# The first store of a split-SiLU kernel as four transfers: partitions by fours, two rows first

## The chip, the cores and the metric

One core of a Trainium2 chip runs the whole program. The metric is the device time of one execution in microseconds (us); eleven executions of the kernel before, in the rounds of e1 to e4, lie between 470.30 and 471.67 us, within 0.3%. Each kernel was also run once under the hardware profiler, and the tables here come from that run. A run more than 1.5% above the fastest of its kernel is called slow and isn't compared.

## The reference

```python
# x: (32, 512, 2048) float32
x1, x2 = x[..., :1024], x[..., 1024:]
out = x1 * (1 / (1 + np.exp(-x1))) * x2      # float32, (32, 512, 1024)
```

That is 134.2 MB in, 67.1 MB out, and two cheap elementwise steps.

## The kernel before

The 16384 rows are cut into 16 tiles of 128 partitions with 8 rows each. A tile is one load of 8 MB (64 KB per partition, in one piece), one silu on ScalarE (ACT), one multiply on VectorE (DVE), and one store of 4 MB (32 KB per partition). SP issues the loads, ACT the stores. There are two input and two output buffers. The first tile is computed in four chunks of two rows, the last is computed and stored in four chunks.

```python
    in_pool = ctx.enter_context(tc.tile_pool(name="in_pool", bufs=2))
    out_pool = ctx.enter_context(tc.tile_pool(name="out_pool", bufs=2))
    ...
    load(0)
    load(1)
    for i in range(n_tiles):
        xt = loaded.pop(i)
        ov = view(out_flat, i)
        ot = out_pool.tile([P, K, half], dt, name="ot")
        if i < n_tiles - 1:
            kc = KC_EDGE if i == 0 else K          # KC_EDGE = 2, K = 8
            for c in range(0, K, kc):
                silu(ot, xt, c, c + kc)            # ACT
                mul(ot, xt, c, c + kc)             # DVE, in place
            nc.scalar.dma_start(out=ov, in_=ot)    # 4 MB
            if i + 2 < n_tiles:
                load(i + 2)                        # 8 MB, nc.sync
            continue
        ...                                        # last tile: four quarters
```

Of the kernel before, what the change touches and what calls it, by code (L numbers as in the profile page):

```python
# [1 line left out]

# [4 lines left out]


def issue_ahead_of_the_first_barrier(nc):




    head, body = nc.main_func.blocks[:2]
    load = next(ins for ins in body.instructions if type(ins).__name__ == "InstDMACopy")
    at = next(
        j for j, ins in enumerate(head.instructions)
        if ins.engine == load.engine and type(ins).__name__ == "InstDrain"
    )
    body.instructions = [ins for ins in body.instructions if ins.name != load.name]  # L20
    head.instructions = head.instructions[:at] + [load] + head.instructions[at:]


@with_exitstack
def kernel(
    ctx: ExitStack,
    tc: tile.TileContext,
    x: bass.AP,
    out: bass.AP,
):  # L30






    nc = tc.nc
    P = nc.NUM_PARTITIONS

    x_flat = x.flatten_outer_dims()  # L40
    out_flat = out.flatten_outer_dims()
    num_rows, in_cols = x_flat.shape
    half = in_cols // 2
    dt = x_flat.dtype

    K = 8
    KC_EDGE = 2
    PLAN = [K] * (num_rows // (P * K))

    in_pool = ctx.enter_context(tc.tile_pool(name="in_pool", bufs=2))  # L50
    out_pool = ctx.enter_context(tc.tile_pool(name="out_pool", bufs=2))

    plan = []
    row = 0
    for k in PLAN:
        plan.append((row, k))
        row += P * k
    assert row == num_rows
    n_tiles = len(plan)

    def view(flat, i):
        row0, k = plan[i]
        return flat[row0:row0 + P * k].rearrange("(p k) d -> p k d", k=k)

    nc.at_finalize(issue_ahead_of_the_first_barrier)


    ctx.enter_context(tc.manual_schedule())

    loaded = {}  # L70

    def load(i):
        xt = in_pool.tile([P, K, in_cols], dt, name="xt")
        nc.sync.dma_start(out=xt[:, :plan[i][1], :], in_=view(x_flat, i))
        loaded[i] = xt

    def silu(ot, xt, c, ce):
        nc.scalar.activation(  # L78
            out=ot[:, c:ce, :],
            in_=xt[:, c:ce, :half],  # L80
            func=mybir.ActivationFunctionType.Silu,
        )

    def mul(ot, xt, c, ce):
        nc.vector.tensor_mul(  # L85
            out=ot[:, c:ce, :],
            in0=ot[:, c:ce, :],
            in1=xt[:, c:ce, half:],
# [9 lines that stand above are left out]
            kc = KC_EDGE if i == 0 else K  # L98
            for c in range(0, K, kc):
                silu(ot, xt, c, c + kc)  # L100
                mul(ot, xt, c, c + kc)
            nc.scalar.dma_start(out=ov, in_=ot)
            if i + 2 < n_tiles:
                load(i + 2)
            continue

        cuts = list(range(0, K, KC_EDGE))
        for n, c in enumerate(cuts + [None, None]):
            if c is not None:
                silu(ot, xt, c, c + KC_EDGE)  # L110
                mul(ot, xt, c, c + KC_EDGE)
            if n >= 2:
                b = cuts[n - 2]
                nc.scalar.dma_start(out=ov[:, b:b + KC_EDGE, :], in_=ot[:, b:b + KC_EDGE, :])


# [1 line left out]
_INS = ['x']  # L118
_OUTS = [((32, 512, 1024), 'float32')]


# [23 lines left out]
```

## Time and profile before

| | before |
|---|---|
| device time, median of 4 runs | 470.56 us |
| span in the profile | 468.6 us |
| loads, stores: share of 16 DMA engines | 66.4%, 33.2% |
| silu of a whole tile, multiply of a whole tile | 7.03 us, 8.69 us |
| distance from tile to tile | 29.0 us |

A tile's silu and multiply take 15.7 us one after the other and fit beside its 29 us; the DMA engines are what is full, at 66.4 + 33.2 = 99.6% of their time. The lines are read in the prediction below. The timeline of the kernel before shows when its first store is issued and when silu of tiles 1 and 2 starts (start, length, engine, line):

```profile
32.70 0.38 ACTq L102 DMA_DIRECT2D out_dram<-ot  x1
44.84 7.03 ACT L78 ACTIVATE ot<-xt 128x8192 f32<-128x8192 f32 x1 [15.70 <-DMA xt<-in_x_dram]
73.81 7.03 ACT L78 ACTIVATE ot<-xt 128x8192 f32<-128x8192 f32 x1 [21.94 <-DMA xt<-in_x_dram]
```

One more view will be needed, the records of single DMA packets in the trace. In them a *packet* is one partition's piece of one transfer (2048 packets of 64 KB for 16 loads of 128 partitions). I sorted them into turns: groups of 16 packets of one queue and size, which I take as one for each of the 16 engines. L64 is a load packet of 64 KB, S32 a store packet of 32 KB, "done" a 4-byte write of 9 ns. Each transfer has 16 of these behind its data (256 for 16 loads, 304 for 19 stores), and I call them its completion: silu of tile 2 starts at 73.81 us, 0.5 us after the last one of load 2 at 73.30. This is the kernel before, with the first and last start of a turn and the shortest, median and longest packet in ns:

```
 61.82.. 62.42  S32   1213 1213 1213
 63.03.. 63.63  L64   2418 2418 2418
 65.44.. 66.04  S done   (store 0)
 65.45.. 66.05  L64   2418 2418 2418
 67.86.. 68.46  S32   1213 1213 1213
 69.07.. 69.67  L64   2418 2418 2418
 71.48.. 72.09  S32   1213 1213 1213
 72.69.. 73.30  L done   (load 2)
 72.70.. 73.30  S32   1213 1213 1213
```

The two queues alternate packet by packet here, a completion write is a turn as well (store 0's at 65.44 us stands alone between the load packets of 63.03 and 65.45), and all 16 engines do the same within 0.6 us.

### The profile page before, as it was taken

Reading aid. Unit: us, or ns where it says so; the run is one execution under the profiler, and the core shown is the slowest. Engines: PE = TensorE matmul, PEld = TensorE weight load, DVE = VectorE, ACT = ScalarE, POOL = GpSimd, SP = SyncE. Lnnn points to the kernel's source line nnn. Section 1 sums busy time; section 2 is a strip of 40 time slices with the busy share of each in tenths; the row PEclk is TensorE's granted clock in tenths of the full one; section 3 lists DMA queues with packets and bytes.
Section 4 is the critical chain, followed back from the end, with each engine's and each line's share of the span. In section 5 each row is a group of like instructions: output and inputs, shape, how many; then the busy total and the mean of one; then the engine's idle time right before and its main releaser. Section 6 shows DMA issues by size and latency. Waiting matters only on the chain.

```text
span 468.6 us, 183 instructions
## 1 busy us (share of the span) xinstructions
DVE 139.5 (30%) x22; ACT 114.3 (24%) x23; POOL 0.2 (0%) x4
## 2 busy tenths in 40 slices
DVE  0070510606115060250702407024070330703333
ACT  1141405023050230503205032050410504105050
POOL 0000000000000000000000000000000000000000
DMA  9899999999999998998999999999999999999998
GB/s 442 386 425 403 439 456 448 403 417 434 448 448 403 448 470 380 448 481 380 481 400 420 478 448 403 403 448 448 448 403 445 434 420 448 431 420 492 394 411 358
DMA packets 5040, 201.33 MB, mean 430 GB/s; under 512 B 560, under 2 KB 560, under 8 KB 560
## 3 DMA queue, kind: packets, MB, share of 16 engines
q1 hardware_dynamic: 2304, 134.22, 66.4%
q10 hardware_dynamic: 2736, 67.11, 33.2%
HBM read 134.22 MB, written 67.11 MB: 430 GB/s over the span
## 4 chain that ended last, share of the span: by engine, by line
DMA 72%; DVE 14%; ACT 11%; DVEq 0%; issue 0%; ACTq 0%
DMA xt<-in_x_dram 72%; DVE ot L85 14%; ACT ot L78 11%; DVEq L140 0%; ACTq L78 0%
## 5 line engine op out<-in xcount | busy, mean ns | idle before, releaser
L85 DVE TENSOR_TENSOR ot<-ot,xt 128x8192 f32<-128x8192 f32 (+1 forms) x22 | 139.5, 6362 | 322.1 <-ACT ot L78 322.1
L78 ACT ACTIVATE ot<-xt 128x8192 f32<-128x8192 f32 (+1 forms) x22 | 113.0, 5163 | 343.0 <-DMA xt<-in_x_dram 343.0
L78 ACT ACT_TABLE_LOAD x1 | 1.3, 1283 | 0.8 <-PEq L129 0.8
L129 POOL MEMSET const-bfloat16-1.0<- 128x1 bf16 x1 | 0.1, 101 | 0.0
L129 POOL MEMSET const-uint8-127<- 128x1 uint8 x1 | 0.1, 101 | 0.0
L129 POOL MEMSET const-float32-0.0<- 128x1 f32 x1 | 0.1, 98 | 0.2 <-issue 0.2
L129 POOL MEMSET const-float32-1.0<- 128x1 f32 x1 | 0.1, 98 | 0.0
## 6 DMA issues: line engine op xcount, KB each, us to landing
out_dram<-ot ACTq DMA_DIRECT2D x15, 4096.0 KB, 34.7
out_dram<-ot ACTq DMA_DIRECT2D x4, 1024.0 KB, 5.7
xt<-in_x_dram SPq DMA_DIRECT2D x16, 42.1
```

What stands on the lines that cost most here:

```text
L78: nc.scalar.activation(out=ot[:, c:ce, :], in_=xt[:, c:ce, :half], func=mybir.ActivationFunctionType.Silu,)
L85: nc.vector.tensor_mul(out=ot[:, c:ce, :], in0=ot[:, c:ce, :], in1=xt[:, c:ce, half:],)
L129: nc = _bacc.Bacc("TRN2", target_bir_lowering=False, num_devices=1)
```

## The change

The intent: the first store begins with small packets and takes more turns, so that the loads get ahead, and the step from loads alone to loads and stores is gentler.

```diff
+    OPENING = [
+        (slice(0, None, 4), slice(0, 2)),
+        (slice(0, None, 4), slice(2, None)),
+        (slice(2, None, 4), slice(None)),
+        (slice(1, None, 2), slice(None)),
+    ]
...
-            nc.scalar.dma_start(out=ov, in_=ot)
+
+            for ps, ks in OPENING if i == 0 else [(slice(None), slice(None))]:
+                nc.scalar.dma_start(out=ov[ps, ks], in_=ot[ps, ks])
```

## The prediction

What rests on nothing that a trace of this case shows is cut from the text on record, and each cut is marked: one paragraph, the first rival (that the choice of partitions makes store packets longer) with the places in the range, the chances and the signs that lean on it, and two guesses at the cause of the slow turn. The sum came to 470.57 - 0.5 + 0.1 = 470.2 us. The -0.5 is the author's estimate, about half of the 1.1 us that the trace shows, and the +0.1 one from the small packets of the tail. The range was 469.5 to 470.9 us without the first rival, and the 0.02 for slower by 2% was for that rival.

> **What bounds the kernel now.** I read the page first: who is busy, and what its chain says.
>
> ```profile
> span 468.6 us, 183 instructions
> ...
> DVE 139.5 (30%) x22; ACT 114.3 (24%) x23; POOL 0.2 (0%) x4
> ...
> q1 hardware_dynamic: 2304, 134.22, 66.4%
> q10 hardware_dynamic: 2736, 67.11, 33.2%
> ...
> DMA 72%; DVE 14%; ACT 11%; DVEq 0%; issue 0%; ACTq 0%
> ```
>
> The compute engines work under a third of the span. Queue q1 carries the loads (issued by SP), q10 the stores (issued by ACT); together their packets fill 66.4 + 33.2 = 99.6% of the time of all 16 DMA engines. The chain gives 25% to DVE and ACT, but a chain is only what released what. To see whether the engines ever ran dry, I cut the span where the traffic changes kind and asked for the DMA share of each stretch (last two columns: share, GB/s).
>
> ```profile
> 0.00:0.90 0.90, 0.00 (x0) 0.12 (x1) 0.20 (x4) 1.00 0.00 0
> 0.90:4.00 3.10, 0.00 (x0) 1.16 (x1) 0.00 (x0) 1.00 0.99 338
> 4.00:35.30 31.30, 8.90 (x4) 7.31 (x4) 0.00 (x0) 1.00 1.01 436
> 35.30:38.80 3.50, 0.00 (x0) 0.00 (x0) 0.00 (x0) 1.00 0.99 300
> 38.80:449.50 410.70, 121.69 (x14) 98.41 (x14) 0.00 (x0) 1.00 1.00 434
> 449.50:456.80 7.30, 4.13 (x2) 6.07 (x4) 0.00 (x0) 1.00 1.00 431
> 456.80:467.10 10.30, 4.77 (x3) 1.24 (x1) 0.00 (x0) 1.00 0.96 407
> 467.10:468.60 1.50, 0.00 (x0) 0.00 (x0) 0.00 (x0) 1.00 0.00 0
> ```
>
> From 0.9 us until the last data at about 467 us the share is 1.00 within the rounding of a packet that crosses a cut. Loads alone (4 to 35 us), loads and stores mixed (39 to 449) and stores alone (449 to 457) all move at 431 to 436 GB/s. (The 407 of the last row comes from a window that ends 0.2 us late and starts late by a packet; 4.19 MB at 434 GB/s are 9.7 us.) So the end is fixed by bytes over one rate: 201.33 MB / 434 GB/s = 463.9 us, plus about 1 us before the first packet, 1.5 us from the last data to the end, and two slow packets. Those two are the first load packets (338 GB/s) and the load packets in flight when the **first store** arrives (300 GB/s): 3.5 x (1 - 300/434) = 1.1 us. The second is the only DMA time that a different first store can recover. The sum, 463.9 + 1 + 1.5 + 0.7 + 1.1 = 468.2, is the span within 0.4.
>
> How the two queues share an engine is seen in one short window just after the first store has come in (queue, packets, MB, share):
>
> ```profile
> DMA packets 32, 1.57 MB, mean 437 GB/s; under 512 B 0, under 2 KB 0, under 8 KB 0
> ...
> q1 hardware_dynamic: 16, 1.05, 67.2%
> q10 hardware_dynamic: 16, 0.52, 33.7%
> ```
>
> That is 38.8 to 42.4 us: every one of the 16 engines took one load packet (64 KB, 2.42 us) and one store packet (32 KB, 1.21 us). A turn is a packet, whatever its size. This is the lever of the change.
>
> [...]
>
> **The change, part by part.** The same 4 MB leave from the same buffer after the same compute; nothing is loaded, computed or issued earlier: the first piece is issued where the whole store was, at 32.70 us. Added: three issues on ACT, about 3 x 0.36 us by the timeline's duration of such an issue, in a stretch where ACT waits for load 1 until 44.84, so hidden. Packets: per engine 8 become 10 (2 of 8 KB, 2 of 24 KB, 6 of 32 KB), and 4 completion writes in place of 1. Small packets cost little: the tail moves its 4 MB in 8 KB packets in about 9.8 us against 9.7 at full rate, 0.1 us for 24 more packets per engine, so 2 more are worth 0.01 us. I allow 0.1 us for all of this.
>
> What moves is the **order**. A completion write takes a turn too (two load packets in succession are seen at 63.0 and 65.4 us, where store 0's completion lies between them). The first store thus takes 14 turns in place of 9, and load packets fill the turns in between. Counted turn by turn from 38.86 us, the start of the first store packet (my estimate, from 2.418, 1.213, 0.91 and 0.31 us for 64, 32, 24 and 8 KB):
>
> - load 1 has one packet left; it ends 0.9 us sooner, since an 8 KB packet stands ahead of it in place of 32 KB. Silu of tile 1 starts near 43.9 in place of 44.84.
> - load 2's completion comes after 9 load packets, 21.8 us, and stores of 0.62 + 1.82 + 4 x 1.21 = 7.3 us: near 67.9, so it lands near 69.0 in place of 73.8.
> - store 0's completion comes after its own 9.7 us and 11 load packets, 26.6 us: near 75.2, where it was at 65.5. It lands near 76.1 in place of 66.4.
>
> The output pool has two buffers, and tile 2 takes the one of tile 0. Its silu will therefore wait for **store 0** (76.1), no longer for load 2 (69.0): 2.3 us later than the 73.81 of now. From there every tile keeps one turn for one turn, so loads stay some 4.8 us ahead, stores some 10 us behind, and each tile's silu waits for the store two back. That looks like a new bound and is none: the engines stay full as long as either queue has work. Load 4 goes out 15.8 us after silu 2 starts (7.0 silu + 8.7 multiply), near 92, while load 3 lasts to near 96; and store 1, issued near 60, lasts past 100. At the end, load 15 lands near 446 in place of 450.7; silu of tile 15 waits for store 13 until about 449.3; the first quarter of the last store is issued near 453.6 (455.0 now), while store 14's eight packets keep the engines to about 458. Today the same handover, store 14's last packet to the first quarter, meets within 0.1 us near 457. So the change adds slack there, with nothing to recover.
>
> The sum: bytes and rate 0; fragments +0.1; the slow turn at the first store between -1.1 and 0. A smaller first packet (8 KB, a quarter) may shorten that turn [...]; I take -0.5. 470.57 - 0.5 + 0.1 = 470.2 us.
>
> **Rivals.** [...] (2) *The new wait starves the DMA.* If loads were issued too late, q1 would run dry; but then q10, with a store and a half queued, runs at the same 434 GB/s. Both would have to be empty. Small. (3) *The tail gains.* A handover gap of a microsecond at 457 would be closed by the longer store queue; the trace shows 431 GB/s up to 456.8 and no hole, so there is no more than 0.1 us. (4) *The whole slow turn goes*: 469.5.
>
> **Range and chances.** Measured runs of before spread over 470.44 to 471.02. [...] 8 in 10: 469.2 to 471.8. Faster by 2% would need 9.4 us, and all DMA time outside bytes over rate is about 5 us, so 0.005. Slower by 2% [...]: 0.02. The rest, 0.975, is within 2%.
>
> **What would show it right or wrong.** The DMA share stays 1.00 in every stretch and 434 GB/s from 39 us on. Silu of tile 1 starts near 44, that of tile 2 near 76; in the view of waits, ACT's waits for loads of x are largely replaced by waits for stores of ot, and the chain names stores. Load 15 lands some 4 to 5 us earlier, the end doesn't move. The stretch around the first store shows whether 300 GB/s has risen. I'm wrong if store packets of 32 KB take clearly over 1.21 us near 45 to 75 us [...], if a stretch shows a DMA share under 0.95, or if the spacing of tiles leaves 29.0 us.

## The result, and the profile after

The changed kernel took 470.57 us (median of 4 runs, 470.31 to 470.69) against 470.56 us. The ratio is 0.9996, with an interval of 0.9981 to 1.0011. Ratios here are the mean time of one kernel's fast runs over that of the other's of the same rounds, so not quite the ratio of the medians. Both profiled runs were fast ones.

The page of the changed kernel shows 80 more packets on the store queue: 2 more data packets and 3 more completion writes for each of 16 engines.

```profile
span 468.5 us, 188 instructions
...
q1 hardware_dynamic: 2304, 134.22, 66.4%
q10 hardware_dynamic: 2816, 67.11, 33.2%
```

The same stretches as in the prediction, for the changed kernel:

```profile
35.30:38.80 3.50, 0.00 (x0) 0.00 (x0) 0.00 (x0) 1.00 0.86 300
38.80:449.50 410.70, 121.69 (x14) 99.65 (x15) 0.00 (x0) 1.00 1.00 433
449.50:456.80 7.30, 6.60 (x3) 6.07 (x4) 0.00 (x0) 1.00 1.00 432
```

The first row is a lesson in reading. The 300 GB/s is the same as before, because a packet counts where it starts, and in both kernels just 16 load packets start in these 3.5 us. The share tells them apart: 0.99 x 3.5 = 3.5 us is the length of one slow load packet before, 0.86 x 3.5 = 3.0 us that of one after. The packet records have 3436 and 2990 ns as the medians, where an ordinary load packet takes 2418. So the slow turn went from 1.02 us over to 0.57.

The timeline of the changed kernel around the first store (start, length, engine, line):

```profile
23.82 8.90 DVE L91 TENSOR_TENSOR ot<-ot,xt 128x2048 f32<-128x2048 f32 x4 [23.82 <-ACT ot L84]
26.15 0.55 ACTq L110 DMA_DIRECT2D out_dram<-ot  x1
27.30 1.89 ACT L84 ACTIVATE ot<-xt 128x2048 f32<-128x2048 f32 x1
32.75 0.33 SPq L80 DMA_DIRECT2D xt<-in_x_dram  x1
32.75 1.78 ACTq L110 DMA_DIRECT2D out_dram<-ot  x3
44.34 7.03 ACT L84 ACTIVATE ot<-xt 128x8192 f32<-128x8192 f32 x1 [15.15 <-DMA xt<-in_x_dram]
51.40 8.69 DVE L91 TENSOR_TENSOR ot<-ot,xt 128x8192 f32<-128x8192 f32 x1 [18.68 <-ACT ot L84]
60.13 0.36 ACTq L110 DMA_DIRECT2D out_dram<-ot  x1
71.27 7.03 ACT L84 ACTIVATE ot<-xt 128x8192 f32<-128x8192 f32 x1 [19.90 <-DMA xt<-in_x_dram]
```

The first piece goes out at 26.15 us and not at 32.7: it holds rows 0 and 1 alone, which the first of the four multiplies finishes (23.82 + 2.29 = 26.11 us), so it waits for that one only. The other three go out where the whole store went before. Its packets of 8 KB run from 30.7 us, when loads are still alone. Silu of tile 2 starts at 71.27, 2.5 us sooner than before (73.81); silu of tile 15 at 448.26 and not 450.73. The data end at 467.13 us in the packet records, before at 467.37. The 2.5 us lead of the loads is not in the end time, because the stores are behind by as much work: after the last load, store 14 has all 8 packets per engine to send, where it had 6 left before.

### The profile page after: what moved, and what is told of

Its sections match the earlier page's. It is cut to its first block, busy times and chain, and to the rows that moved or that the text cites. A ratio compares the mean times of both kernels' runs of the same rounds, so it can differ in the third digit from the quotient of the medians.

```text
span 468.5 us, 188 instructions
## 1 busy us (share of the span) xinstructions
DVE 139.5 (30%) x22; ACT 114.3 (24%) x23; POOL 0.2 (0%) x4
## 4 chain that ended last, share of the span: by engine, by line
DMA 72%; DVE 14%; ACT 11%; DVEq 0%; issue 0%; ACTq 0%
DMA xt<-in_x_dram 72%; DVE ot L91 14%; ACT ot L84 11%; DVEq L148 0%; ACTq L84 0%
## 5 line engine op out<-in xcount | busy, mean ns | idle before, releaser
L91 DVE TENSOR_TENSOR ot<-ot,xt 128x8192 f32<-128x8192 f32 (+1 forms) x22 | 139.5, 6362 | 319.6 <-ACT ot L84 319.6
L84 ACT ACTIVATE ot<-xt 128x8192 f32<-128x8192 f32 (+1 forms) x22 | 113.0, 5163 | 340.5 <-DMA xt<-in_x_dram 340.5
```

What stands on the lines that cost most here:

```text
L84: nc.scalar.activation(out=ot[:, c:ce, :], in_=xt[:, c:ce, :half], func=mybir.ActivationFunctionType.Silu,)
L91: nc.vector.tensor_mul(out=ot[:, c:ce, :], in0=ot[:, c:ce, :], in1=xt[:, c:ce, half:],)
```

## The experiments

Twelve kernels ran. I call **offset** the number of load packets between the completion of a load and the next completion of a store, counted in the turns of one tile after another. A tile has 8 load packets, so it runs from 0 to 8. It is 6 in the kernel before (above: "S done" comes two load packets ahead of "L done"), and 8 in the changed kernel, where the store's completion takes the turn just ahead of the load's. The first eight kernels were made without this idea, the last four because of it. The medians are over all runs, and those of e3, e5 and e8 include one slow run; the ratios are of fast runs alone. The intervals of e5, e7, x2 and x4 lie clear of 1.

| kernel | median, us | ratio to before (95%) | offset |
|---|---|---|---|
| e1_after: the changed kernel again | 470.66 | 0.9995 (0.9983 to 1.0007) | 8 |
| e2_late4: four pieces, none early | 470.61 | 0.9994 (0.9982 to 1.0007) | 2 |
| e3_rows: 2 rows, then 6, all partitions | 471.06 | 1.0009 (0.9987 to 1.0030) | 3, then mostly 0 |
| e4_contig: neighbouring partitions | 470.61 | 0.9993 (0.9980 to 1.0006) | 8 |
| e5_less_load: half of load 7 left out | 465.08 | 0.9853 (0.9827 to 0.9879) | 8, then 0 |
| e6_half_mul: half of the multiplies | 470.73 | 0.9994 (0.9981 to 1.0007) | 8 |
| e7_store0_late: first store 8 us later | 480.10 | 1.0198 (1.0185 to 1.0212) | 1 |
| e8_all_four: every store in four pieces | 497.50 | 1.0555 (1.0523 to 1.0587) | changing |
| x1_late_two: e7, first store in halves | 470.95 | 1.0005 (0.9990 to 1.0020) | 2 |
| x2_three_late: three pieces, none early | 480.63 | 1.0210 (1.0193 to 1.0227) | 1 |
| x3_halves: first store in halves | 470.79 | 1.0004 (0.9990 to 1.0019) | 7 |
| x4_back: x2, then store 5 in halves | 476.08 | 1.0112 (1.0091 to 1.0133) | 1, later mostly 2 |

### e1_after

No edit: the changed kernel again, in five rounds.

> The changed kernel once more, in five rounds, to narrow the interval. Theory (the 16 DMA engines are full from the first packet to the last, so only the slow turn at the first store can be won): the data end 0.2 to 0.3 us sooner in the two traces, so the ratio is 0.9990 to 1.0000, silu of tile 1 near 44.3 and of tile 2 near 71.3. Rival (the earlier start of the first store is a real gain of a microsecond that four runs could not resolve): ratio 0.998 or less.

0.9995 with an interval of 0.9983 to 1.0007: no gain that five rounds can resolve, and none of a microsecond and more would have hidden. Silu of tile 1 starts at 44.54, of tile 2 at 71.47.

### e2_late4

```diff
-        (slice(0, None, 4), slice(0, 2)),
-        (slice(0, None, 4), slice(2, None)),
+        (slice(0, None, 4), slice(6, 8)),
+        (slice(0, None, 4), slice(0, 6)),
```

> The same four pieces, but the first holds rows 6 and 7, which are ready last, so that none can be issued before 32.7 us. This is what the prediction assumed. Theory: the turn count of the prediction holds here: silu of tile 2 near 76 us, released by store 0 and no longer by load 2 (which lands near 69); time within 0.3% of the kernel before. The slow load packet near 36 us: at most as long as in the changed kernel (3.0 us) if a small first store packet shortens it, 3.4 us if not. Rival (early issue is what keeps the changed kernel level, and fragments cost): this one is slower by 1 us or more.

Level, 470.61 us. This is the kernel that the prediction had in mind, and its turn count comes out. The timeline of e2:

```profile
32.85 2.50 ACTq L110 DMA_DIRECT2D out_dram<-ot  x4
42.12 7.03 ACT L84 ACTIVATE ot<-xt 128x8192 f32<-128x8192 f32 x1 [12.83 <-DMA xt<-in_x_dram]
...
57.90 0.36 ACTq L110 DMA_DIRECT2D out_dram<-ot  x1
75.70 7.03 ACT L84 ACTIVATE ot<-xt 128x8192 f32<-128x8192 f32 x1 [26.55 <-DMA out_dram<-ot]
```

Silu of tile 2 waits for store 0 and starts at 75.70 (76.1 predicted). In the packet records load 2 completes from 67.6 us on (67.9 predicted), store 0 from 74.9 (75.2 predicted). Only silu of tile 1 is off: 42.12, where 43.9 was predicted, because the count forgot the second 8 KB packet, which saves another 0.9 us (309 ns in place of 1213), and the shorter slow turn saves the rest. ACT now spends its waiting on stores, as the waits of e2 show, and the end is where it was:

```profile
ACT ot L84 <- DMA out_dram<-ot: 307.4, 14, 26.6
ACT ot L84 <- DMA xt<-in_x_dram: 32.8, 2, 19.9
```

307 us of waiting for another transfer, and not 0.1% in the time: here a wait of an engine that isn't the bound changed its name for nothing. The long load packet at the first store is spread over two turns here (2516 ns at 35.5 us, 2807 at 41.2, in the median), 0.49 us over in all, with nothing issued early. So a small first packet was enough to make the slow turn shorter (0.49 us over, 1.02 in the kernel before); what the slow turn is, I didn't find.

### e3_rows

```diff
-    OPENING = [... four pieces ...]
+    OPENING = [
+        (slice(None), slice(0, 2)),
+        (slice(None), slice(2, None)),
+    ]
```

> Two transfers, no striding: rows 0 and 1 of all partitions, issued near 26 us, then rows 2 to 7. 16 packets per engine (8 of 8 KB, 8 of 24 KB). Theory: time within 0.3% of both kernels; first store packets near 30.7 us as in the changed kernel; early issue comes from the rows and not from the partitions. More turns in the early stretch (8 small packets each with a load packet between), so store 0 lands later than in the changed kernel, silu of tile 2 after 75 us. Rival (the strided partitions matter): this differs from the changed kernel by more than 1 us.

Fast runs: 473.42, 470.49, 470.46, 471.64, 470.43, and a slow one of 482.72. 473.42 stands out. The profile is of that run. In it only 28 load packets after 60 us take over 2.5 us, but one engine falls 2 us behind the others near 67 us and a few later on, and the end waits for the last: the last store's completion writes run from 466.6 to 470.1 us, against 466.8 to 467.4 in the kernel before. The first piece was issued at 26.42, as expected, and silu of tile 2 started at 80.00. So load 4 was issued only at 95.8 us, as load 3 was ending, and on most engines stores took the turns until it came: this is where offset 3 ended.

Which engines lose time after that can be followed, since on an engine each packet starts within a few ns of the end of the one before it (3 to 5 ns in the kernel before, from 60 to 440 us). Twelve engines went on at offset 0 and one at 2; none of their load packets took over 2.5 us between 104 us and the end. Three engines were at offset 1 for a part of the run, and 26 of the 28 slow packets are theirs, mostly one per tile. The two that were at offset 1 from about 244 us on lost 1.8 and 2.1 us between 232 and 440 us. So in this run engines at offset 1 fell behind even though the others were not at it.

### e4_contig

```diff
+        (slice(0, 32), slice(0, 2)),
+        (slice(0, 32), slice(2, None)),
+        (slice(32, 64), slice(None)),
+        (slice(64, 128), slice(None)),
```

> The same four pieces by size, over neighbouring partitions: 0 to 31 (2 rows, then 6), 32 to 63, 64 to 127. [...] Rival (an engine's rate is all that counts, whichever partitions it reads): packets stay at 1.21 us and the time within 0.3%.

Level, 470.61 us, and every 32 KB packet of partitions 32 to 63 and of 64 to 127 took 1213 ns, as in the kernel before. The theory had longer store packets for neighbouring partitions; no trace shows what it rested on. With these packets it falls, so does rival (1) of the prediction, and with them the reason I had seen for the stride of four. Which partitions a piece holds made no difference here; how many packets and pieces there are, does, as x2 will show (2.1%). That is for store packets between load packets; a store of 64 partitions alone wasn't run.

### e5_less_load

```diff
-        nc.sync.dma_start(out=xt[:, :plan[i][1], :], in_=view(x_flat, i))
+        kl = K // 2 if i == 7 else K
+        nc.sync.dma_start(out=xt[:, :kl, :], in_=view(x_flat, i)[:, :kl, :])
```

(Tile 7 is then computed in halves, both from the rows that were loaded. The result is wrong.)

> The changed kernel with only half of tile 7 loaded (4.19 MB less; the compute of tile 7 uses the half that is there twice, so the result is wrong on purpose). Theory (bytes over 434 GB/s set the end): 9.7 us less, so near 460.9 us, ratio near 0.979. Rival (the compute on the chain of waits sets a part of the end): the saving is under 7 us.

The fast runs were 461.96, 465.19 and 464.97; the kernel before had a median of 471.17 us in these rounds. By the ratio that is 6.9 us less, where 9.7 was expected; one run alone comes near, 9.2 us less. The interval, 5.7 to 8.2 us less, leaves the 9.7 out, so the theory's number failed. By the letter the rival ("under 7 us") has it, but e6 speaks against its reason, and what took the rest is open. The profile (469.77 us) isn't compared. What it shows by itself is a warning: the short load moved the offset from 8 to 0, and from there on the engines were up to 4 us apart and many load packets longer than 2418 ns (the page has 432 GB/s in the mean of slices 3 to 20 and 419 in that of 21 to 39, all of them nine tenths busy or more).

### e6_half_mul

```diff
-                mul(ot, xt, c, c + kc)
+                mul(ot, xt, c, c + (kc if i == 0 else K // 2))
```

(A wrong result.)

> The changed kernel with VectorE multiplying only half the rows of tiles 1 to 14 (wrong result on purpose). The chain of waits gives DVE 14% of the span, and this takes about 4.3 us out of each of 14 tiles, 60 us in all. Theory: the end stays within 0.3%, since loads and stores are only issued earlier into queues that are already full. Rival (the chain is the bound): every second tile lies on the chain, so some 30 us less.

```profile
span 468.6 us, 188 instructions
...
DVE 79.7 (17%) x22; ACT 114.3 (24%) x23; POOL 0.2 (0%) x4
```

DVE lost 59.8 us of work (139.5 to 79.7), and the span is 468.6. The chain's 14% for DVE was worth nothing: the chain is a path, and the DMA queues beside it were full (share 1.00, 433 GB/s from 76 to 449 us).

### e7_store0_late

The kernel before, with the first store moved behind silu of tile 1:

```diff
                 silu(ot, xt, c, c + kc)
+                if i == 1:
+                    nc.scalar.dma_start(out=first[0], in_=first[1])
                 mul(ot, xt, c, c + kc)
-            nc.scalar.dma_start(out=ov, in_=ot)
+            if i == 0:
+                first = (ov, ot)
+            else:
+                nc.scalar.dma_start(out=ov, in_=ot)
```

> The kernel before, with the whole first store held back until ACT has started silu of tile 1, so issued near 45 us and not at 32.7. Theory: loads run alone in the meantime at the same rate, so the time is within 0.3%; tile 2 waits for store 0. The slow load packet moves with the store, to about 47 to 50 us, and is again near 3.4 us, since the first store packet is 32 KB. Rival for the slow packet (it belongs to the issue of load 2 at 32.7 us): it stays near 35.5 us. Rival for the time (the earlier first store is worth what it is earlier): 10 us slower.

Here the theory failed: 480.10 us, 2% slower. The rival for the time named nearly this number ("10 us slower") for another reason, which x1 will test. On the slow packet the theory held: it moved with the store, to 42.8 us, and was again 3438 ns. (47 to 50 was expected: the store was issued at 41.11 and not near 45, since load 1, alone on the engines, ended sooner.)

From 76 to 449 us the DMA engines of e7 are as busy as those of the kernel before, and move less. First row the kernel before, second e7:

```profile
76.00:449.00 373.00, 113.00 (x13) 89.19 (x13) 0.00 (x0) 1.00 1.00 434
```

```profile
76.00:449.00 373.00, 112.99 (x13) 89.10 (x13) 0.00 (x0) 1.00 1.00 427
```

Share 1.00 in both. A packet's time is busy time also when the packet is slow, so a full share, here with 434 and 427 GB/s, is no proof of a full rate. In the packet records of e7 the load packets are slow and the engines drift apart (columns as above):

```
 98.25.. 98.92  L done   (load 3)
 99.47..100.14  L64   2418 2418 2418
101.88..102.55  S done   (store 1)
101.89..102.56  L64   2418 2542 2716
104.30..105.21  S32   1213 1213 1213
105.51..106.42  L64   2418 2528 2625
```

375 load packets of 2048 took over 2.5 us (32 in the kernel before, all of them in the first and the slow turn); the excess over 2418 ns sums to 7.9 us per engine, against 1.7. Tiles are 29.57 us apart (silu at 102.88 and, eleven tiles on, at 428.10), against 28.99.

### e8_all_four

```diff
-            for ps, ks in OPENING if i == 0 else [(slice(None), slice(None))]:
+            for ps, ks in OPENING:
```

> The changed kernel with all 15 stores of 4 MB in the same four pieces: measures what fragments cost, and drives the stores behind the loads tile after tile. Theory: 30 more packets per engine and 45 more completion writes cost at most 0.1 us a tile, so 0 to 1.5 us slower; loads fall dry at times, and the DMA share stays 1.00 all the same, since stores are queued. Rival (loads issued late starve the engines once every tile waits for a store): 5 us or more slower, with a DMA share under 0.97 in the middle.

The rival was right: 497.50 us. Each store takes 14 turns to a load's 9, so by the count stores fall behind anew at each tile, until silu waits for a store (249.6 us in all in the profile), the multiply for silu (352.2 us) and the next load for the multiply (330.7 us). A stretch of e8 and its longest wait for a transfer (the profile is of a run called slow, 502.53 us, so I read from it only that the share falls and who waits for whom; the sizes are those of that run alone):

```profile
187.00:204.00 17.00, 7.37 (x2) 7.03 (x1) 0.00 (x0) 1.00 0.73 299
```

```profile
ACT ot L84 <- DMA out_dram<-ot: 249.6, 7, 39.6
```

The prediction's "the engines stay full as long as either queue has work" may hold, but e8 shows stretches in which the engines aren't full (share 0.73 above). My reading, from the count of turns and not from a measured lag: the lag of the stores grows with each tile until the two buffers on each side no longer cover it. What a fragment costs by itself can't be read from e8.

### x1_late_two

e7 again, with the late store in two pieces, for one more turn:

```diff
-                    nc.scalar.dma_start(out=first[0], in_=first[1])
+                    for ps in (slice(0, None, 2), slice(1, None, 2)):
+                        nc.scalar.dma_start(out=first[0][ps], in_=first[1][ps])
```

> The held-back first store of e7 (2% slower), now as two transfers of 64 partitions each (even, odd), which adds one completion write and so one turn. In e7 every store's completion comes one load packet after a load's completion (offset 1); here it should come two after (offset 2, as in e2_late4, which was level). Theory of the offset (the time hangs on which load packet lies beside which store packet, not on when the first store starts): 470.6 us within 0.3%, tiles 29.0 us apart, load packets at 2418 ns. Rival (the late first store itself costs): about 480 us as e7.

470.95 us, level. The store is as late as in e7 (issued at 41.40, e7 at 41.11), and the 9 us that e7 lost to the kernel before are gone. So it wasn't the lateness. 36 load packets took over 2.5 us (e7: 375), and tiles are 28.99 us apart.

### x2_three_late

The reverse: e2 was level at offset 2; one turn less makes it 1.

```diff
+        (slice(0, 32), slice(6, 8)),
+        (slice(0, 32), slice(0, 6)),
+        (slice(32, 128), slice(None)),
```

> Like e2_late4 (all pieces issued after 32.7 us, level in time), with three pieces instead of four: partitions 0 to 31 in rows 6 and 7, then rows 0 to 5, then partitions 32 to 127. 10 packets and 3 completion writes, 13 turns and not 14, so offset 1 as in e7. Theory of the offset: slow like e7, 475 to 481 us, with load packets over 2.5 us after the first completion of a store and tiles over 29.2 us apart. Rival (e7 was slow only because its store was late): 470.6 us within 0.3%.

480.63 us, slower by 2.1%. Same stretch of the trace as above, for x2:

```profile
76.00:449.00 373.00, 112.99 (x13) 90.15 (x13) 0.00 (x0) 1.00 1.00 427
```

345 load packets took over 2.5 us, the excess sums to 9.2 us per engine, and at the end the first and last engine are 3.8 us apart (last completion writes from 473.4 to 477.2) in place of 0.6. Tiles are 29.61 us apart. In e2 and x2 ACT waits for stores alike (307.4 and 317.8 us), so that wait is not the cause.

### x3_halves

```diff
+        (slice(0, None, 2), slice(None)),
+        (slice(1, None, 2), slice(None)),
```

> The plainest split: the first store as two transfers of 64 partitions (even, odd), both issued at 32.7 us. 10 turns where the kernel before has 9, so the offset goes from 6 to 7 load packets. Neither theory has a number for offset 7: if it is level with the kernel before, offset 1 is an exception; if slower by over 1%, the offsets of the kernel before and the changed kernel are good ones among bad ones. Slow packet at the first store as before, 3.4 us, since the first packet is 32 KB.

470.79 us, level at offset 7. The slow turn at the first store is 3365 ns in the median, as before, since the first packet is 32 KB again.

### x4_back

x2, with the store of tile 5 in two halves as well:

```diff
+                else [(slice(0, None, 2), slice(None)), (slice(1, None, 2), slice(None))] if i == 5
```

> x2_three_late (offset 1, 2.1% slower), with the store of tile 5 in two transfers, which adds one turn, so that from there on the offset is 2. By then the first and the last engine are about 3 us apart. Theory A (the pairing at offset 1 is what is slow, at each tile anew): tiles come back to 29.0 us apart from about tile 8 on, and the kernel lies near 475 us. Theory B (offset 1 only drives the engines apart, and engines that are apart stay slow whatever the offset): tiles stay at 29.4 to 29.6 us and the kernel at 479 to 481 us.

476.08 us, near theory A's 475. The starts of silu in x4, the last one ahead of the added turn, the first behind it, and that of the last whole tile:

```profile
194.19 7.03 ACT L83 ACTIVATE ot<-xt 128x8192 f32<-128x8192 f32 x1 [22.67 <-DMA out_dram<-ot]
...
226.30 7.03 ACT L83 ACTIVATE ot<-xt 128x8192 f32<-128x8192 f32 x1 [25.08 <-DMA out_dram<-ot]
...
429.60 7.03 ACT L83 ACTIVATE ot<-xt 128x8192 f32<-128x8192 f32 x1 [22.05 <-DMA out_dram<-ot]
```

Before it, tiles were 29.65 us apart (105.23 to 194.19, three tiles); behind it they are (429.60 - 226.30) / 7 = 29.04 us apart, though the engines stay 3 us apart to the end. So engines that are apart are not slow for that alone, and theory B falls. The records don't name engines, but as far as the chains of packets can be followed, six of the 16 slipped back to offset 1 within a few tiles. Between 232 and 440 us their load packets took 1.8 to 2.5 us in all over the usual length, those of the eight engines that stayed at offset 2 0.2 to 0.5 us, and those of x2, with all engines at offset 1, 3.6 to 5.3 us. So the six were slow again, about half as much as in x2; that the tiles kept their 29 us all the same would fit if they wait for the last engine and that one was at offset 2, but this was not shown.

### What follows, and what stays open

Shown: with the same bytes, compute and buffers, offset 1 costs 2% by two independent routes (e7 and x2), and one added turn takes the cost away from each (x1, e2) or stops it midway (x4). Within one run, too, the engines at offset 1 have the slow packets and those at 0 or 2 hardly any (e3, x4). Offsets 2, 6, 7 and 8 are level (6 is the kernel before; the ratios of the others are 0.9993 to 1.0005). Offset 0 is unsettled: the engines at 0 in e3's profile lost nothing, but e3 was level in three runs only, and in e5's slow run the load packets were long after it had come to 0. Offset 3 was held for two tiles only (e3); 4 and 5 didn't occur as lasting ones. Not shown: why offset 1 is slow; no run here tests a cause. No version was found that beats both kernels; the medians of those at the level of the kernel before lie between 470.57 and 471.06 us.

## Why the prediction was right or wrong

**The bound: right.** e6 takes 60 us off DVE and moves nothing. (The size of the bytes' share isn't confirmed: e5 saved 6.9 us where bytes over 434 GB/s gave 9.7.) e1 bounds the effect of the change to between -0.17% and +0.07%.

**The slow turn at the first store: right in kind, the term a little large.** It was put at -0.5 us, with 0.1 back for fragments. It measured -0.45 (1.02 to 0.57 us over the ordinary packet). Smaller delays at the first small packets took part of that back (13 load packets near 28 and 31 us over by 0.1 to 0.3 us). All packets together take 466.85 us per engine after and 466.98 before, and the data end 0.24 us sooner. Predicted 470.2, measured 470.57: the traces show 0.24 us of the forecast 0.4, and the timings can't tell either from zero (the interval of the ratio is -0.9 to +0.5 us).

**"Nothing is loaded, computed or issued earlier: the first piece is issued where the whole store was, at 32.70 us": wrong.** It went out at 26.15. I took the store as one with its buffer; the program waits for the rows that a transfer reads, and rows 0 and 1 are ready after the first of four multiplies, at 26.11 us. The diff shows the slice and the code the four chunks; both were before me.

**The turn count: right as arithmetic but for one packet, wrong for this kernel, for the reason just named.** With the first pieces sent while loads were alone, store 0 completes near 70.1 and not 75.2, together with load 2, silu of tile 2 starts at 71.27 and not 76, and the waits for loads stay (340.5 us) where I had waits for stores replace them. Load 15 completes 2.6 us sooner (from 447.10 us on, before from 449.69), where 4 to 5 were forecast. With early issue undone (e2), its times for load 2, store 0 and tile 2 came out within 0.4 us; that for tile 1 was 1.8 us late, by a packet left out of the count.

**Rivals.** The first, store packets made longer by the choice of partitions: no, by e4 and by packets of 1213 ns. Starvation by the new wait: not here; but in e8, with every store in four pieces, the share does fall (0.73 from 187 to 204 us). A gain in the tail: none, as argued. The whole slow turn gone: no, 0.57 of its 1.02 us stayed.

**What the prediction had no idea of** is the one thing that could have made it wrong by 10 us. It took 434 GB/s as given for any order of turns. The change moves the offset from 6 to 8, two level ones. With one piece fewer and no early issue it would have been 1, and the answer "2% slower" (x2). The chance of 0.02 for slower was right by luck as much as by reasoning: nothing in the trace of the kernel before shows that such an order exists.

## What to carry to other kernels

In these kernels, with a DMA share of 1.00 from first packet to last, what a new order of transfers could win was what the load packets took over their usual 2418 ns: 1.7 us per engine in the kernel before, 7.9 in e7. Find such packets in the records and add them up before trying. A share of 1.00 didn't prove the rate (434 GB/s before, 427 in e7), so compare GB/s over equal stretches too. And a split or an extra transfer shifted the turns of everything behind it, which cost 2.1% (x2) or took 2% away (x1 against e7): when such an edit costs some per cent for no reason in sight, add or take one turn elsewhere before giving it up.
